# One of two halves gets its own buffers, the gates become plain fp32 and come last: the mixing stage of a two-block network

## The chip, the cores and the metric

One Trainium2 chip, one core. The time is device microseconds of one execution; the median of several runs is compared. The profile is one execution taken by the hardware profiler.

## The reference

A sequence of 256 tokens, width 1024, goes through a first block of two layers (feed-forward, a hybrid attention mixer, feed-forward) and then through a second block, whose mixing sublayer the change is about. It projects the modulated input `u` with one weight matrix `w_in` (1024 x 6032) into columns for three things:

```python
a_lat, b_lat, gates_lat = split(u_lat @ w_in, ...)
oa, _ = gdn_branch(a_lat, state_a)               # gated DeltaNet, 4 heads of 128
ob, _ = rwkv_branch(to_col_major(b_lat), state_b) # RWKV-7, 8 heads of 64
y = (sigmoid(g_a) * (oa @ w_o_a) + sigmoid(g_b) * (ob @ w_o_b)) @ w_out
```

Both branches run over the tokens in two directions and start from states that the same branches computed on a context of 256 tokens. RWKV first mixes each column with its neighbours, `cols + (0.5*(left + right) - cols) * mu`, then builds per token a decay, a key, a removal vector and a value, and runs a linear recurrence. A hierarchical mixture of experts (32 experts, the most of the weights) follows, and a last norm.

## The kernel before

The program is written as Python that emits instructions; a planner orders them. Every instruction has a priority (the order in which the program emits it; `high_priority(n)` puts a stretch ahead by n), and the planner, with its own model of durations, lets each engine take the first ready one. Each engine then runs its list in that fixed order. On-chip memory comes from pools on two stacks ("left", "right"); a tile in a place that was used before waits until the old tile's last reader is done. A tag with `bufs=n` is a ring of n buffers.

Matrix products with weights are done in three matmuls of reduced fp32: `split_w` (L90) makes a high part on ScalarE (L132) and a low part on VectorE (L133), and `mm3` (L99) multiplies low by high, high by low, high by high (L102 to L104). `norm_pair` (L175) gives `u` as such a pair, `hh` and `hl`.

`mix` (L2182) runs the stage. `begin` computes `u` and stores both parts to DRAM as `u_lat`. `rwkv_proj` projects v, k, w, r in this order (15 column blocks of 128; `shifted`, L1399, does the neighbour mix in `evict`). Then `rwkv` (L1434) works on four pairs of heads, in two halves of two pairs. In `rwkv_half` (L1491), `first` (L1506) builds for a pair and a direction the decays (tanh, a scan, two exponentials) and the factors AR and BK; `second` (L1556) multiplies them on TensorE, masks the products on VectorE (L1569 Mak, L1571 Ur, L1574 Mr) and transposes; there are four such stages in a half. Then the 64x64 triangular matrices are inverted (`inverse`, L951: transposes on VectorE, 15 steps of substitution L975 and L977, then products of blocks on TensorE), and a chain of four chunks (L1625 on) carries the state and accumulates the outputs `yr`. `rwkv_out` normalizes a half into `ob`.

All of this has high priority. The buffers AR, BKT, U, R1, Mr and SV exist once, so half 1's writes wait for half 0's readers. Below that priority come, in the order of the program, `gdn_z` and `gdn_proj` (17 blocks; the convolution's taps are L1093), `gates_ahead` (L2217) and `gdn` (L1157). `gates_ahead` computes the 2048 gate columns ahead of their use: 8 groups, each over 8 blocks of `u` reloaded from `u_lat` (L2226), with weights split by ScalarE (L2229) and GpSimd (L2230), the tanh stored to DRAM. `gdn` prepares factors for four heads (L1246), inverts 128x128 matrices by the same `inverse`, and runs two chunks; `gdn_out` gives `oa` (L1760). PSUM has 8 banks: two each for tags "g" and "s" (RWKV), three for "a" (GDN), one for "w" (gates). `merge` (L2251) then multiplies `oa`, `ob` with their output weights (branch a first), scales with the gates, and projects.

The context's RWKV (`ctx_second`) uses the same functions without outputs, beside a feed-forward of the first block.

Of the kernel before, what the change touches and what calls it, by code (L numbers as in the profile page):

```python
# [31 lines left out]
class Core:  # L32
# [142 lines left out]
    def norm_pair(self, pool, x, rs, A, B=None, keep=None, save=None):  # L175
# [7 lines left out]
        for t in range(2):  # L183
# [17 lines left out]
            if save is not None:  # L201
                for i, v in enumerate((hh, hl)):
                    nc.sync.dma_start(out=save[:, i, :, ts], in_=v[:, :, ts].bitcast(F32))
# [719 lines left out]
class Block2:  # L923
    def __init__(self, k, a, rows, pool):
        self.k, self.a, self.R, self.cst = k, a, rows, pool
        tc, nc, ctx = k.tc, k.nc, k.ctx
# [22 lines left out]


    def inverse(self, U, nb, size):  # L951
# [6 lines left out]
        assert nb == B  # L958

        t = pool.tile([P, B, 32], F32, tag="t2", name="Ut", bufs=self.t2)  # L960
        for q in range(4):
            bs, cb = slice(32 * q, 32 * q + 32), 32 * q % size
            nc.vector.transpose(t[bs].rearrange("p a b -> p (a b)"),
                                U[bs, :, cb:cb + 32].rearrange("p n (h c) -> p c h n", h=2))
        W = pool.tile([P, B, B], F32, tag="inv", name="Ub", bufs=3)
        nc.vector.tensor_scalar(W, t[:, :, 0:B], self.halves[:, 0:1], None, op0=OP.mult)
# [35 lines left out]
        pq = bmm("g", B, [(b, U[st[b], :, diag[b]], DD[st[b], :, 0:B]) for b in range(4)])  # L1002
# [8 lines left out]
        pq = bmm("g", 32, [(b + 1, U[st[b], :, off[b]], DD[st[b]]) for b in (0, 2)])  # L1011
        nc.vector.tensor_copy(Q[st[1]], pq[st[1]])
        nc.scalar.activation(Q[st[3]], pq[st[3]], AF.Copy)
        for b in range(4):
            if b % 2:
                nc.gpsimd.tensor_copy(U[st[b], :, diag[b]], DT[st[b]])
            else:
                nc.scalar.activation(U[st[b], :, diag[b]], DT[st[b]], AF.Copy)
# [3 lines left out]
        nc.vector.tensor_copy(U[st[0], :, off[0]], px[st[0]])  # L1022
        nc.scalar.activation(U[st[2], :, off[2]], px[st[2]], AF.Copy)
# [35 lines left out]
    def proj(self, u, w, start, n, evict):  # L1059
# [5 lines left out]
        for f0 in range(0, n, 256):  # L1065
            pg = k.ps("g", [P, 2, T], "pg")
            for g0 in range(f0, min(f0 + 256, n), wide):
                m = min(wide, n - g0)
                wr = k.raw(w[:, start + g0: start + g0 + m].rearrange("(c p) f -> p c f", p=P), [P, KC, m])
                for h0 in range(0, m, P):  # L1070
                    mm = min(P, m - h0)
                    fi = (g0 + h0 - f0) // P
                    for c0 in range(0, KC, cs):
# [83 lines left out]
    def gdn(self, cols, s0, with_out, name, Sout=None):  # L1157
# [88 lines left out]
        def factors(h):  # L1246
# [8 lines left out]
            for dn in range(4):  # L1255
                nc.vector.tensor_scalar(E[:, dn], gb[:, dn], col[:, dn, h:h + 1], 0.0, op0=OP.subtract, op1=OP.min)
            nc.scalar.activation(E, E, AF.Exp)
# [102 lines left out]
class Rwkv(Block2):  # L1360
# [3 lines left out]
    def rwkv_setup(self):  # L1364
# [11 lines left out]
        self.mstr = c.tile([P, 64], F32, name="mstr")  # L1376
        self.minc = c.tile([P, 2, 64], F32, name="minc")
        for h in range(2):
            b = slice(64 * h, 64 * h + 64)
            one = k.ones[b, 0:64]  # L1380
            nc.gpsimd.affine_select(self.mstr[b], one, pattern=[[1, 64]], base=0, channel_multiplier=-1,
                                    compare_op=OP.is_gt, fill=0.0)
            nc.gpsimd.affine_select(self.minc[b, 0], one, pattern=[[1, 64]], base=0, channel_multiplier=-1,
                                    compare_op=OP.is_ge, fill=0.0)
            nc.gpsimd.affine_select(self.minc[b, 1], one, pattern=[[-1, 64]], base=63, channel_multiplier=-1,
                                    compare_op=OP.is_ge, fill=0.0)
        nv = c.tile([P, 12 + 15 + 16], F32, name="rwc")
        self.mu = R["rwkv_mu_2"]
# [10 lines left out]
    def shifted(self, u, w, start, nch, mu0, colmajor, out):  # L1399
# [3 lines left out]
        def evict(i, m, pg):  # L1403
            pad = pool.tile([P, 2, T + 2], F32, tag="t2", name="pad2", bufs=self.t2)
            nc.gpsimd.memset(pad[:, :, 0:T + 2:T + 1], 0.0)
            for j in range(m):
                src, dst = pg[:, j], pad[:, j, 1:T + 1]
                if colmajor:
                    src = src.rearrange("p (r c) -> p c r", r=4)
                    dst = dst.rearrange("p (c r) -> p c r", r=4)  # L1410
                nc.scalar.activation(dst, src, AF.Copy)
            x = pad[:, :m, 1:T + 1]
            s = pool.tile([P, 2, T], F32, tag="t2", name="shs", bufs=self.t2)
            nc.gpsimd.tensor_tensor(s[:, :m], pad[:, :m, 0:T], pad[:, :m, 2:T + 2], op=OP.add)
            nc.vector.scalar_tensor_tensor(s[:, :m], s[:, :m], 0.5, x, op0=OP.mult, op1=OP.subtract)
            for j in range(m):
                nc.vector.scalar_tensor_tensor(out[:, i + j], s[:, j], self.mu[:, mu0 + i + j:mu0 + i + j + 1],
                                               pad[:, j, 1:T + 1], op0=OP.mult, op1=OP.add)
        self.proj(u, w, start, nch * P, evict)

    def rwkv_part(self, name, u, w, colmajor, lows=3):

        start, n, tag = dict(v=(1024, 4, "vT"), k=(512, 4, "kTr"), w=(1536, lows, "lo"), r=(0, 4, "rT"))[name]
        t = self.keep.tile([P, n, T], F32, name=tag)
        self.shifted(u, w, 2064 + start, n, self.MU[name], colmajor, t)
# [4 lines left out]
    def rwkv_proj(self, u, w, colmajor):  # L1430

        return tuple(self.rwkv_part(name, u, w, colmajor) for name in "vkwr")

    def rwkv(self, cols, S0, with_out, name, Sout=None, ob=None):  # L1434


# [8 lines left out]
        kk = pool.tile([P, 4, T], F32, tag="kk", name="kk")  # L1445
# [12 lines left out]
        rkT = pool.tile([72, T], F32, tag="rkT", name="rkT")[64:72]  # L1458
# [5 lines left out]
        out = None  # L1464
        for hf in range(2):

            SV = pool.tile([P, 2, 4, 4, 64], F32, tag="SV", name="SV")
            for d in range(2):
                vh = vT[:, 2 * hf:2 * hf + 2]
                if d == 1:  # L1470
                    vr = pool.tile([P, 2, T], F32, tag="t2", name="vTb", bufs=self.t2)
                    nc.vector.tensor_copy(vr, rev(vh))
                    vh = vr
                for t in range(2):
                    pt = k.ps("s", [P, 2, P], "ptv")
                    for p in range(2):
                        nc.tensor.transpose(pt[:, p], vh[:, p, t * P:(t + 1) * P], k.ident)
                    for q in range(2):
                        for h in range(2):
                            i = pt[64 * q:64 * q + 64, :, 64 * h:64 * h + 64]  # L1480
                            o = SV[64:128, h, 2 * t + q, 2 * d:2 * d + 2]
                            if h == 0:
                                nc.scalar.activation(o, i, AF.Copy)
                            else:
                                nc.vector.tensor_copy(o, i)
            out = self.rwkv_half(hf, kT, rT, lo, kk, SV, None if S0 is None else S0[:, hf],
                           with_out, name + str(hf), None if Sout is None else Sout[:, hf], vT, ob, out)
        if with_out:
            out()

    def rwkv_half(self, hf, kT, rT, lo, kk, SV, S0, with_out, name, Sout, vT, ob, before):  # L1491
# [3 lines left out]
        AR = pool.tile([P, 4, 4, na, 64], F32, tag="AR", name="AR")  # L1495
        BKT = pool.tile([P, 4, nb, P], F32, tag="BKT", name="BKT")
        U = pool.tile([P, 16, 64], F32, tag="U", name="Ur")
        R1 = pool.tile([P, 4, 4, 64], F32, tag="R1", name="R1")
        gam = pool.tile([P, 4, 4], F32, tag="gam", name="gam")
        Mr = None  # L1500
        if with_out:
            Mr = pool.tile([P, 4, 2, 4, 64], F32, tag="Mr", name="Mr")
            bon = pool.tile([P, 2, 4], F32, tag="bon", name="bon")
        kds = {}

        def first(pl, d):  # L1506
# [12 lines left out]
            kd = pool.tile([P, T], F32, tag="kd%d" % d, name="kdr", bufs=2)  # L1519
            nc.vector.tensor_scalar(kd, th[:, 1], self.kah[:, p:p + 1], self.kac[:, p:p + 1],  # L1520
                                    op0=OP.mult, op1=OP.add)
            nc.gpsimd.tensor_tensor(kd, kd, kT[:, p], op=OP.mult)
            kds[pl, d] = kd
            nc.vector.tensor_scalar(th, th, 0.5, 0.5, op0=OP.mult, op1=OP.add)
            nc.gpsimd.tensor_tensor(th[:, 1], th[:, 1], kk[:, p], op=OP.mult)
# [4 lines left out]
            ee = pool.tile([P, 2, 4, 64], F32, tag="t2", name="ee", bufs=self.t2)  # L1530
            ep, em = ee[:, 0], ee[:, 1]
            cum4 = cum.rearrange("p (c t) -> p c t", t=64)
            nc.scalar.activation(ep, cum4, AF.Exp, scale=-EMH)
            nc.scalar.activation(em, cum4, AF.Exp, scale=EMH)
            nc.vector.tensor_copy(gam[:, :, pd], ep[:, :, 63])
# [4 lines left out]
            kkd = nat(kk[:, p])  # L1540
            aa = AR[:, pd, :, 0]
            nc.vector.scalar_tensor_tensor(aa[:, :, 1:], kkd[:, :, 1:], -1.0, ep[:, :, :63],
                                           op0=OP.mult, op1=OP.mult)
            nc.vector.tensor_scalar(aa[:, :, 0:1], kkd[:, :, 0:1], -1.0, None, op0=OP.mult)
            if with_out:
                rv = rT[:, p].rearrange("p (c t) -> p c t", t=64)
                if d == 0:
                    nc.gpsimd.tensor_tensor(AR[:, pd, :, 1], rv, ep, op=OP.mult)
                else:
                    nc.gpsimd.tensor_tensor(AR[:, pd, :, 1], revd(rv, (1,)), revd(ep, (2,)), op=OP.mult)  # L1550
            BK = pool.tile([P, 4, 2, 64], F32, tag="t2", name="BK", bufs=self.t2)
            nc.vector.tensor_tensor(BK[:, :, 0], nat(th[:, 1]), em, op=OP.mult)
            nc.vector.tensor_tensor(BK[:, :, 1], nat(kd), em, op=OP.mult)
            return BK

        def second(pl, d, BK):  # L1556

            pd = 2 * d + pl
            bs = [slice(0, 64), slice(64, P)]
# [871 lines left out]
```

## Time and profile before

| | |
|---|---|
| median of 3 runs | 2396.19 us (2391.33 to 2402.87) |
| profiled execution | 2390.7 us, its span 2389.0 us |
| TensorE (matmul) busy | 2249.9 us (94%), 19065 instructions |
| VectorE | 1689.7 us (71%) |
| ScalarE | 1199.8 us (50%) |
| GpSimd | 344.1 us (14%) |
| mean granted TensorE clock | 0.953 |

The clock is a share of full speed (1.00 is 2.4 GHz, 0.50 is 1.2 GHz). PE is TensorE, PEld its weight load, DVE VectorE, ACT ScalarE, POOL GpSimd, SP the engine that issues most DMAs. A matmul's recorded duration holds its way through the array, so durations overlap, and spacing tells the rate. A matmul of plain fp32 operands leaves two records, one of the reduced kind one. The mixing stage runs from 1616 us, when the first block ends, to about 2053 us; the experts follow to the end.

### The profile page before, as it was taken

How to read it: one execution, taken by the hardware profiler on the slowest of the kernel's cores; microseconds unless marked ns; L12 is line 12 of the kernel's file. 1: busy time of each engine (PE TensorE's matmuls, PEld its weight loads, DVE VectorE, ACT ScalarE, POOL GpSimd, SP SyncE). 2: the span in 40 equal slices, each digit the busy share in tenths (PEclk: the TensorE clock that was granted, in tenths of full speed). 3: DMA queues.
4: the chain of work that ended last, by engine and by line, in shares of the span. 5: the costliest groups of instructions: out<-in, count | busy, mean ns of one | idle time of the engine just before them, and what ended most of it. 6: DMA issues, size and time to landing. Idle time of an engine off the chain costs nothing. (4 is left out here: it accounts for less than half of the span.)

```text
span 2389.0 us, 46279 instructions
## 1 busy us (share of the span) xinstructions
PE 2249.9 (94%) x19065; PEld 2041.7 (85%) x19065; DVE 1689.7 (71%) x2796; ACT 1199.8 (50%) x1919; POOL 344.1 (14%) x465
## 2 busy tenths in 40 slices
PE   7999999999999999999999999998989887899997
PEld 6999988897889888888888979998877777799996
DVE  6775575766665674675856668886885866789997
ACT  5554455555443543544554554443553313477775
POOL 2000112121200100100122210002245511000000
PEclk9999999999999989999999999998988668899999
DMA  9676344455434334342545468986445415699992
GB/s 327 223 248 202 111 150 143 140 166 188 142 125 163 132 112 152 128 142 68 173 130 166 143 211 299 331 285 185 125 133 161 146 40 193 239 374 351 353 352 98
DMA packets 325166, 450.91 MB, mean 189 GB/s; under 512 B 16122, under 2 KB 253236, under 8 KB 324564
## 3 DMA queue, kind: packets, MB, share of 16 engines
q1 hardware_dynamic: 324276, 447.06, 55.9%
q8 instruction: 152, 2.49, 0.4%
q0 software_dynamic: 672, 0.82, 0.3%
q14 instruction: 66, 0.54, 0.1%
HBM read 438.09 MB, written 9.76 MB: 187 GB/s over the span
## 5 line engine op out<-in xcount | busy, mean ns | idle before, releaser
L133 DVE TENSOR_TENSOR wl<-raw,wh 128x1024 fp32r<-128x1024 f32 (+1 forms) x703 | 860.0, 1230 | 364.4 <-ACT wh L132 355.2
L132 ACT ACTIVATE wh<-raw 128x1024 fp32r<-128x1024 f32 (+1 forms) x703 | 730.5, 1043 | 465.8 <-PE pg L104 189.5
L102 PE MATMUL pg<-hh,wl 128*128 128x256 f32 x2176 | 627.9, 289 | 4.9 <-DVE wl L133 4.4
L103 PE MATMUL pg<-hl,wh 128*128 128x256 f32 x2176 | 625.9, 288 | 0.4 <-DVE hl L133 0.4
L104 PE MATMUL pg<-hh,wh 128*128 128x256 f32 x2176 | 625.8, 288 | 0.0
L102 PEld LDWEIGHTS pg<-hh,wl 128*128 128x128 f32 x2176 | 420.1, 193 | 17.2 <-issue 6.0
L103 PEld LDWEIGHTS pg<-hl,wh 128*128 128x128 f32 x2176 | 420.0, 193 | 11.1 <-issue 6.6
L104 PEld LDWEIGHTS pg<-hh,wh 128*128 128x128 f32 x2176 | 420.1, 193 | 7.8 <-issue 6.4
L102 PE MATMUL ph<-wh,m0t 128*128 128x256 f32 x512 | 146.4, 286 | 0.0
L102 PE MATMUL acc<-wh,ul 128*128 128x512 f32 x352 | 137.9, 401 | 8.7 <-DVE ul L133 7.0
L103 PE MATMUL ph<-wl,m0t 128*128 128x256 f32 x512 | 144.2, 282 | 0.1
L104 PE MATMUL ph<-wh,m0t 128*128 128x256 f32 x512 | 143.7, 281 | 0.0
L104 PE MATMUL acc<-wh,uh 128*128 128x512 f32 x352 | 140.7, 400 | 0.0
L103 PE MATMUL acc<-wl,uh 128*128 128x512 f32 x352 | 140.4, 399 | 0.0
L103 PE MATMUL acc<-wl,hh 128*128 128x512 f32 (+2 forms) x320 | 120.5, 377 | 0.0
L104 PE MATMUL acc<-wh,hh 128*128 128x512 f32 (+2 forms) x320 | 120.4, 378 | 0.0
L102 PE MATMUL acc<-wh,hl 128*128 128x512 f32 (+2 forms) x320 | 116.9, 381 | 0.5 <-DVE hl L133 0.5
L103 PEld LDWEIGHTS ph<-wl,m0t 128*128 128x128 f32 x512 | 96.5, 189 | 1.2 <-DVE wl L133 0.4
L104 PEld LDWEIGHTS ph<-wh,m0t 128*128 128x128 f32 x512 | 96.5, 188 | 0.5
L102 PEld LDWEIGHTS ph<-wh,m0t 128*128 128x128 f32 x512 | 96.7, 189 | 0.1
L454 ACT ACTIVATE sg<-pg 128x256 f32<-128x256 f32 x80 | 30.8, 385 | 127.4 <-PE pg L104 123.8
L1705 DVE SCALAR_TENSOR_TENSOR adacc<-raw,silu_c,adacc 128x512 f32<-128x512 f32 x112 | 83.4, 747 | 15.3 <-DMA raw<-in_ada_w_dram 14.7
(712 smaller groups left out, 4214.5 us busy)
## 6 DMA issues: line engine op xcount, KB each, us to landing
raw<-in_ffn_w_gu_dram SPq DMA_DIRECT2D x88, 1024.0 KB
raw<-in_w_in_dram SPq DMA_DIRECT2D x56, 1024.0 KB
raw<-in_ffn_w_down_dram SPq DMA_DIRECT2D x44, 1024.0 KB
raw<-in_w_gate_dram SPq DMA_DIRECT2D x32, 1024.0 KB
raw<-in_moe_w_gate_dram SPq DMA_DIRECT2D x32, 1024.0 KB
raw<-in_moe_w_up_dram SPq DMA_DIRECT2D x32, 1024.0 KB
raw<-in_moe_w_down_dram SPq DMA_DIRECT2D x32, 1024.0 KB
raw<-in_ada_w_dram SPq DMA_DIRECT2D x48, 512.0 KB
```

The lines of the kernel that those rows point to most:

```text
L102: t.matmul(out, lhs[1], rhs[0], start=start, stop=False)
L103: t.matmul(out, lhs[0], rhs[1], start=False, stop=False)
L104: return t.matmul(out, lhs[0], rhs[0], start=False, stop=stop)
L132: return (nc.scalar.activation(h, src, AF.Copy), nc.vector.tensor_tensor(l, src, h.bitcast(F32), op=OP.subtract))
L133: nc.vector.tensor_tensor(l, src, h.bitcast(F32), op=OP.subtract))
L454: nc.scalar.activation(sg, pg[:, 0], AF.Silu)
L1705: nc.vector.scalar_tensor_tensor(acc, wv, sc, acc, op0=OP.mult, op1=OP.add)
```

## The change

Six things, all in the second block. (1) RWKV's halves: `rwkv_half` takes its buffers from a pool given to it, builds factors and products at once and returns a function `solve` for the rest; the two halves' pools are separate, the second laid where the projections' memory was. Solves have priorities of their own. (2) Gates: `norm_pair` also adds the two parts of `u` to a full fp32 tile `uf` on GpSimd, the gates use plain fp32 matmuls on unsplit weights, `u_lat` goes, and they are emitted after GDN. (3) Masked products: the two halves of heads are laid so that one operation masks all (`UM`, `mask2`). (4) Factors: key and removal factor as one tile `X`, the first column of AR without an operation of its own; the shift as `out*(1-mu) + 0.5*mu*(left+right)`. (5) In the mixing stage (`lean`) several scalings and GDN's subtraction move from VectorE to ScalarE. (6) Order and rings: w, k, r, v; `gdn_proj` before `gdn_z`; the projections' split weights have 2 buffers, not 3.

```diff
 norm_pair:
+            if full is not None:
+                nc.gpsimd.tensor_tensor(full[:, js, ts], hh[:, js, ts].bitcast(F32), hl[:, js, ts].bitcast(F32), op=OP.add)
 inverse (U becomes at(b), one tile for each half of partitions):
-        nc.vector.tensor_scalar(W, t[:, :, 0:B], self.halves[:, 0:1], None, op0=OP.mult)
+        self.scaled(W, t[:, :, 0:B], self.halves[:, 0:1])      # ScalarE if lean, else VectorE
-            for h in range(2):
-                nc.vector.tensor_scalar(t[:, :, B * h:B * h + B], yv, self.halves[:, h:h + 1], None, op0=OP.mult)
+            nc.vector.tensor_scalar(t[:, :, 0:B], yv, self.halves[:, 0:1], None, op0=OP.mult)
+            self.scaled(t[:, :, B:], yv, self.halves[:, 1:2])
 gdn factors, if lean:
-                nc.vector.tensor_scalar(E[:, dn], gb[:, dn], col[:, dn, h:h + 1], 0.0, op0=OP.subtract, op1=OP.min)
+                    nc.scalar.activation(E[:, dn], gb[:, dn], AF.Relu, scale=-1.0, bias=col[:, dn, h:h + 1])
 shifted:
                 nc.scalar.activation(dst, src, AF.Copy)
+                nc.scalar.activation(o, src, AF.Copy, scale=self.mu1[:, mu0 + i + j:mu0 + i + j + 1])
-            nc.vector.scalar_tensor_tensor(s[:, :m], s[:, :m], 0.5, x, op0=OP.mult, op1=OP.subtract)
 rwkv_half, first:
-            nc.gpsimd.tensor_tensor(kd, kd, kT[:, p], op=OP.mult)
-            nc.vector.tensor_scalar(th, th, 0.5, 0.5, op0=OP.mult, op1=OP.add)
-            nc.gpsimd.tensor_tensor(th[:, 1], th[:, 1], kk[:, p], op=OP.mult)
+            for o, i in ((f[:, 0], th[:, 1]), (th[:, 0], th[:, 0])):
+                if self.lean:
+                    nc.scalar.activation(o, i, AF.Copy, scale=0.5, bias=0.5)
...
+            for h in range(2):
+                o = X[hb[h]]
+                nc.gpsimd.tensor_tensor(o if h == 0 else revd(o, (1,)), f[hb[h]], kkT[hb[h], p], op=OP.mult)
-            nc.vector.tensor_copy(gam[:, :, pd], ep[:, :, 63])
+            nc.scalar.activation(gam[:, :, pd], cum4[:, :, 63], AF.Exp, scale=-EMH)
-            nc.vector.tensor_tensor(BK[:, :, 0], nat(th[:, 1]), em, op=OP.mult)
-            nc.vector.tensor_tensor(BK[:, :, 1], nat(kd), em, op=OP.mult)
+            nc.vector.tensor_tensor(BK.rearrange("p c j t -> p j c t"), Xn if d == 0 else revd(Xn, (2, 3)),
+                                    em.unsqueeze(1).to_broadcast([P, 2, 4, 64]), op=OP.mult)
 rwkv_half, second:
-                nc.vector.tensor_tensor(Mak[64:128], pm[64:128, :, 0], ..., op=OP.mult)
-                nc.vector.tensor_tensor(U[b, 4 * pd:4 * pd + 4], pm[0:64, :, 0], ..., op=OP.mult)
-                    nc.vector.tensor_tensor(Mr[:, pd, h], pm[:, :, 1], ..., op=OP.mult)
+                nc.vector.tensor_tensor(UM[h][:, 4 * pd:4 * pd + 4], pm,
+                                        self.mask2[:, d, 0:na].unsqueeze(1).to_broadcast([P, 4, na, 64]), op=OP.mult)
 mix:
-            wp = Weights(proj.enter_context(k.pool("uw", "right")), 2048, 2, 1024, 3)
+            wp = Weights(proj.enter_context(k.pool("uw", "right")), 2048, 2, 1024, 2)
                 with k.tc.high_priority(100000):
-                    self.rwkv(cols, self.Sb, True, "rl", None, ob)
+                    kk = self.rwkv_keys(cols, True)
+                    solve = [half(0, seta)]
                 with k.use(**G), k.pool("gp", "right") as self.pool:
-                    self.gdn_z(u, w, oa)
                     gcols = self.gdn_proj(u, w, True)
+                    self.gdn_z(u, w, oa)
             proj.close()
+            setb = right.enter_context(k.pool("rb", "right"))
+            with k.tc.high_priority(100000), k.use(**G):
+                solve.append(half(1, setb))
+            with k.tc.high_priority(200000):
+                solve[0]()
+            with k.tc.high_priority(100000):
+                solve[1]()
-            with k.pool("gm", "right") as self.pool, k.use(W=Weights(gf, 256, 4, 256, 2), **G):
-                self.gates_ahead(gf, a["w_in_2"][0][:, 3984:6032])
+            with k.pool("gm", "right") as self.pool, k.use(W=Weights(gf, 512, 4, 0, 0), **G):
                 self.gdn_out(self.gdn(gcols, self.Sa, True, "gl"), oa)
+                self.gates_ahead(a["w_in_2"][0][:, 3984:6032])
 gates_ahead:
-                    u = pool.tile([P, 2, 2, T], F32, tag="u", name="u", bufs=2)
-                    nc.sync.dma_start(out=u, in_=self.u_lat[:, :, c:c + 2])
-                nc.scalar.activation(ws[0], wr, AF.Copy)
-                nc.gpsimd.tensor_tensor(ws[1], wr, ws[0].bitcast(F32), op=OP.subtract)
-                    k.mm3(pg[:, j], ...)
+                    nc.tensor.matmul(pg[:, j], wr[:, c % 2, j * P:j * P + P], self.uf[:, c],
+                                     start=c == 0 and j == 0, stop=c == KC - 1 and j == 1)
```

The context's RWKV takes (3) and (4) too, with the scalings left on VectorE.

## Rows read from the trace of the kernel before

**Rows 1.** Windows: us, then busy us (instructions) of PE, PEld, DVE, ACT, POOL; clock, DMA
```profile
1635.00:1755.00 120.00, 116.96 (x953) 109.94 (x951) 91.90 (x164) 60.46 (x104) 34.22 (x39) 0.99 0.44 133
1755.00:1858.00 103.00, 86.44 (x1274) 74.96 (x1273) 65.67 (x158) 42.96 (x125) 53.51 (x65) 0.87 0.59 176
1858.00:1922.00 64.00, 52.13 (x424) 44.76 (x423) 54.05 (x113) 20.92 (x51) 30.46 (x41) 0.70 0.42 123
1922.00:1995.00 73.00, 62.71 (x1460) 56.58 (x1459) 43.37 (x110) 13.99 (x39) 6.11 (x10) 0.71 0.23 74
1995.00:2053.00 58.00, 47.84 (x281) 42.55 (x282) 39.80 (x42) 22.78 (x29) 9.34 (x9) 0.87 0.71 248
```

**Rows 2.** Windows of 10 us, where two inverses' small matmuls run alone
```profile
1940.00:1950.00 10.00, 8.63 (x418) 8.37 (x411) 3.14 (x8) 0.00 (x0) 0.00 (x0) 0.50 0.28 104
```

**Rows 3.** Timeline of VectorE (start us, us, ...): first and last of each half's preparation
```profile
1702.96 0.41 DVE L1520 TENSOR_SCALAR kdr<-th,rwc 128x256 f32<-128x256 f32 x1
...
1757.09 0.43 DVE L1574 TENSOR_TENSOR Mr<-pm,minc 128x256 f32<-128x256 f32 x1
...
1863.49 0.41 DVE L1520 TENSOR_SCALAR kdr<-th,rwc 128x256 f32<-128x256 f32 x1
...
1914.53 0.42 DVE L1574 TENSOR_TENSOR Mr<-pm,minc 128x256 f32<-128x256 f32 x1
```

**Rows 4.** Timeline of TensorE: half 0's last outputs, which read SV and Mr
```profile
1847.40 0.97 PE L1619 MATMUL yr<-SV,Mr 128*64 128x64 f32 x16
```

**Rows 5.** Timeline of VectorE: GDN's inverse and output; from 1922.35 half 1's inverse
```profile
1857.67 0.69 DVE L1268 TENSOR_TENSOR U<-Eb,pk 128x512 f32<-128x512 f32 x1
...
1868.49 0.14 DVE L975 TENSOR_TENSOR Pb<-Ub,Yb 128x1 f32<-128x1 f32 x1
...
1900.47 0.38 DVE L977 TENSOR_REDUCE Yb<-Pb 128x15 f32<-128x225 f32 x1
...
1921.95 0.47 DVE L1003 TENSOR_SCALAR Q<-ps_inv,halves 128x256 f32<-128x256 f32 x1
1922.35 0.15 DVE L975 TENSOR_TENSOR Pb<-Ub,Yb 128x1 f32<-128x1 f32 x1
...
1935.19 0.39 DVE L977 TENSOR_REDUCE Yb<-Pb 128x15 f32<-128x225 f32 x1
...
1941.58 0.48 DVE L1003 TENSOR_SCALAR Q<-ps_inv,halves 128x256 f32<-128x256 f32 x1 [0.74 <-PE ps_inv L996]
...
1953.83 0.68 DVE L1045 COPY U<-ps_inv 64x512 f32<-64x512 f32 x1 [1.64 <-PE ps_inv L1044]
...
1994.34 0.75 DVE L1760 SCALAR_TENSOR_TENSOR oa<-pt,rowcols,oa 128x512 f32<-128x512 f32 x1 [0.72 <-PE pt L1758]
```

**Rows 6.** Timelines of TensorE and ScalarE: the end of half 1's output, then branch b
```profile
2009.18 0.66 PE L1807 MATMUL pt<-ident,yrw 128*128 128x128 f32 x4 [3.06 <-DVE yrw L1803]
...
2009.65 0.66 ACT L1809 ACTIVATE ob<-pt 128x256 f32<-128x256 f32 x2 [2.39 <-PE pt L1807]
...
2013.65 0.55 PE L102 MATMUL pb<-o,wl 128*128 128x256 f32 x1 [3.82 <-DVE merged L251]
```

**Rows 7.** The projections' matmuls by tile: ns min/median/max, first and last start
```profile
L104 PE MATMUL pg<-hh,wh x256: 277/283/420, 1634.4 to 1755.0; 128*128 128x256 f32 x124, 128*16 128x256 f32 x4
```

**Rows 8.** Window with the gates' matmuls alone (those that read tile u)
```profile
1755.00:1922.00 167.00, 69.83 (x376) 0.80 0.52 156
```

**Rows 9.** Plain fp32 matmuls of 128x128 by 256: by line, then two in sequence
```profile
L804 PE MATMUL sbs<-sbw,m_lt x16: 377/379/382, 376.8 to 1228.0; 128*128 128x256 f32 x16
...
376.78 0.60 PE L804 MATMUL sbs<-sbw,m_lt 128*128 128x256 f32 x2
```

**Rows 10.** Groups by form, 1615 to 2000 us: xcount | busy us, mean ns | idle before
```profile
L2230 POOL TENSOR_TENSOR wl<-raw,wh 128x256 fp32r<-128x256 f32 x64 | 50.0, 785 | 61.6 <-ACT wh L2229 59.3 <-issue 2.1
L133 DVE TENSOR_TENSOR wl<-raw,wh 128x1024 fp32r<-128x1024 f32 x34 | 42.7, 1261 | 22.5 <-ACT wh L132 22.4
L132 ACT ACTIVATE wh<-raw 128x1024 fp32r<-128x1024 f32 x34 | 35.7, 1055 | 19.4 <-PE pg L104 13.9 <-DVE kk L1449 3.6 <-DMA raw<-in_w_in_dram 1.8
L1569 DVE TENSOR_TENSOR Mak<-pm,mstr 64x256 f32<-64x256 f32 x16 | 6.8, 428 | 3.7 <-PE pm L1563 3.3
L1574 DVE TENSOR_TENSOR Mr<-pm,minc 128x256 f32<-128x256 f32 x16 | 6.6, 415 | 0.1
```

More of the change, by code (lines that the diff above doesn't have):

```diff
@@ L173, in rms, with norm_pair @@
         return self.pow(pool, v, "%sr%d" % (name, t))
-    def norm_pair(self, pool, x, rs, A, B=None, keep=None, save=None):
+    def norm_pair(self, pool, x, rs, A, B=None, keep=None, full=None):
         nc = self.nc
@@ L1072, in proj @@
                     fi = (g0 + h0 - f0) // P
+                    if not isinstance(u, (tuple, list)):
+                        for c in range(KC):
+                            k.nc.tensor.matmul(pg[:mm, fi], wr[:, c, h0:h0 + mm], u[:, c], start=c == 0, stop=c == KC - 1)
+                        continue
                     for c0 in range(0, KC, cs):
@@ L1463, in rwkv @@
             nc.vector.tensor_tensor(kk[:, p], kk[:, p], pb, op=OP.mult)
-        out = None
+        return kk
+    def rwkv(self, cols, S0, name, Sout):
+        kk = self.rwkv_keys(cols, False)
         for hf in range(2):
[L1467 to L1487, printed above, removed]
@@ L1488, in rwkv, with rwkv_half @@
-        if with_out:
-            out()
-    def rwkv_half(self, hf, kT, rT, lo, kk, SV, S0, with_out, name, Sout, vT, ob, before):
-        k, nc, pool, R = self.k, self.k.nc, self.pool, self.R
+            self.rwkv_half(hf, cols, kk, S0, False, name + str(hf), Sout[:, hf], None, self.pool)()
+    def rwkv_half(self, hf, cols, kk, S0, with_out, name, Sout, ob, sets):
+        k, nc, pool, R = self.k, self.k.nc, self.pool, self.R
+        vT, kT, lo, rT = cols
+        S0 = None if S0 is None else S0[:, hf]
+        kkT = kT
+        SV = sets.tile([P, 2, 4, 4, 64], F32, tag="SV", name="SV")
+        for d in range(2):
+            vh = vT[:, 2 * hf:2 * hf + 2]
+            if d == 1:
+                vr = pool.tile([P, 2, T], F32, tag="t2", name="vTb", bufs=self.t2)
+                nc.vector.tensor_copy(vr, rev(vh))
+                vh = vr
+            for t in range(2):
+                pt = k.ps("s", [P, 2, P], "ptv")
+                for p in range(2):
+                    nc.tensor.transpose(pt[:, p], vh[:, p, t * P:(t + 1) * P], k.ident)
+                for q in range(2):
+                    for h in range(2):
+                        i = pt[64 * q:64 * q + 64, :, 64 * h:64 * h + 64]
+                        o = SV[64 - 64 * h:128 - 64 * h, h, 2 * t + q, 2 * d:2 * d + 2]
+                        if h == 0:
+                            nc.scalar.activation(o, i, AF.Copy)
+                        else:
+                            nc.vector.tensor_copy(o, i)
@@ L1604, in rwkv_half @@
         second(*last)
-        if before is not None:
-            before()
-        XT = self.inverse(U, 16, 64)
-        if with_out:
-            gate = self.rwkv_gate(hf, bon, vT, lo[:, 2])
-        if with_out:
-            yp = [k.ps("g", [P, 2, 2, 64], "yr") for _ in range(2)]
-        def outputs(c, lhs, rhs, first, last):
-            for d in range(2):
-                cn = 3 - c if d else c
-                for pl in range(2):
-                    for h in range(2):
-                        nc.tensor.matmul(yp[h][64 * (cn % 2):64 * (cn % 2) + 64, cn // 2, pl], lhs(h, 2 * d + pl),
-                                         rhs(h, 2 * d + pl), start=first and pl == 0, stop=last and pl == 1)
@@ L1670 @@
+        return solve
 class Tail(Rwkv):
@@ L2089, in ctx_store @@
         if c is not None:
-            self.ctx[name] = self.dram.tile(list(c.shape), F32, name="c" + c.name)
+            c = c[:, :, 1] if name == "k" else c
+            self.ctx[name] = self.dram.tile(list(c.shape), F32, name="c%s" % name)
             self.k.nc.sync.dma_start(out=self.ctx[name], in_=c)
@@ L2104, in ctx_load @@
             if d is not None:
-                t = self.keep.tile(list(d.shape), F32, name="cl%s" % i)
-                self.k.nc.sync.dma_start(out=t, in_=d)
+                n = list(d.shape)
+                t = self.keep.tile(n[:2] + [2] + n[2:] if i == "k" else n, F32, name="cl%s" % i)
+                self.k.nc.sync.dma_start(out=t[:, :, 1] if i == "k" else t, in_=d)
             out.append(t)
```

272 lines of the change are left out of this document (146 added, 126 removed).

## The prediction

> **What bounds the kernel now.** I read the page's busy shares and its 40 slices first: TensorE is busy nearly everywhere, and the slices where it and its clock fall lie between two thirds and nine tenths of the span. That is the mixing stage of the second block, the only place where the change alters the order of work. Then I read this stage by parts [rows 1]. From 1635 to 1755 us the projections run: TensorE is busy 117.0 of 120 us at clock 0.99, VectorE 91.9. From 1755 to 1995 us it is another regime: TensorE 201.3 of 240 us (86.4 + 52.1 + 62.7), VectorE 163.1, ScalarE 77.9, the clock only 0.70 to 0.87, and at 0.50 where chains of small matmuls run alone [rows 2]. No engine is full there. What ends this part is two chains: the second RWKV half, and gated DeltaNet (GDN) with its triangular inverse.
>
> The VectorE timeline shows why they are late. Half 0's factors and products run from 1703 to 1757, half 1's only from 1863 to 1915 [rows 3]. They are the same work, but half 1 writes the buffers that half 0 reads until 1848.4 [rows 4]. It so falls on top of GDN's inverse. GDN's last product is written at 1857.7; the 15 steps of its substitution take from 1868.5 to 1900.9, because half 1's instructions stand between them; the next result is used at 1922.0. Half 1's own inverse, with nothing between, needs 1922.4 to 1935.6 for the steps, and is at that same point at 1941.6. GDN's last correction is written at 1954.5, its output ends at 1995.1 [rows 5], and half 1's output ends later still, at 2010.3 [rows 6].
>
> **The change part by part.** The profiled execution took 2390.7 us (its span 2389.0 and 1.7 around it); the sum is made against it. The median of the runs is 2396.19, 0.2% more.
>
> *Separate buffers.* Half 1 gets its own set, laid where the projections' input and weights were, so it can start when their last matmul ends, at 1755.0 [rows 7], not 1863: some 105 us earlier. What is late next is GDN, so only its part of the collision counts. The steps shrink from 32.4 us (1868.5 to 1900.9) to the 13.2 us of half 1's own: 19.2. The stretch from there to the next use shrinks from 21.1 to 6.0: 15.1. Together **-34**.
>
> The following block products (1922.0 to 1954.5, 32.5 us) ran at clock 0.5 beside half 1's inverse. At the higher of the two clock levels (2.4 against 1.2 GHz) they could take half, without any change they take the same: 0 to -16. I take **-8**: the gates, which now come last, will lie between them and keep TensorE at work, but half 1's solve may still be near.
>
> *GDN's preparation (1768 to 1858)* loses the gates' matmuls and gets half 1's preparation beside it instead, with three PSUM banks for both and RWKV first. The gates hold TensorE for 69.8 us between 1755 and 1922 [rows 8]; half 1's preparation is 53 us long now. VectorE has room: 65.7 of 103 us busy [rows 1]. I take 0, bounds -20 and +53 (all of half 1's preparation put in front).
>
> *Half 1's output.* The merge waits for it now: TensorE stands idle 3.1 and 3.8 us for its last steps [rows 6]. With half 1 done first this goes: **-7**.
>
> *Gates in plain fp32.* They were 128 products of three matmuls; a 128x256 one takes 0.12 us at full clock (953 in 117.0 us [rows 1]), so 46 us. A plain fp32 product of this shape is recorded as two matmuls: one lasts 0.38 us, two together 0.60, so each adds 0.22 [rows 9]. 128 x 2 x 0.22 = 56 us. TensorE gets 10 us more, and since it must now fit into a shorter stretch I count all of it: **+10** (bounds 0, hidden, and +56, all at the end). The loss of 64 splits, 50.0 us on GpSimd [rows 10], and of the reloads of the input counts nothing: neither engine nor queue ends this stage. On SP the gates now issue 32 loads of weights and 8 stores, emitted after GDN; the merge's first weights stand behind them in that queue, which costs nothing while the gates are done before GDN, and belongs to the first rival if not.
>
> The Trainium skill, page "Perfetto Trace Analysis", section "Engine Utilization", puts the output rate of an fp32 matmul at half the usual one. Taken per product that would make the gates cheaper, an estimated 28 us, and the sum 28 us lower. The trace agrees per matmul (0.22 against 0.12) but shows two per product, so I stay with the row.
>
> *Projections.* Three buffers for split weights become two. Each part is split by ScalarE in 1.06 us and then VectorE in 1.26 [rows 10], 2.3 in sequence, while TensorE needs 24 x 0.12 = 2.9 for a part. The slack is 0.6 us, and VectorE is 77% busy [rows 1]: a part that meets a group of RWKV's operations waits. If each of GDN's 17 parts lost 2 us it is +34; if the planner fills the holes with gates, nothing. I take 0: the gates are plain matmuls that need no split and can fill them, and the projections then hand work forward.
>
> *VectorE's smaller work.* The shift loses one of its operations (7), each of the 8 stages loses 8 of 14 (the masked products go from six to two), 9 scalings and 16 subtractions move to ScalarE (busy 60.5 of 120 and 43.0 of 103 us [rows 1]). That is 96 operations less, 40 us at the 0.42 us of a 128x256 one [rows 10]; 24 that remain double in length, at 0.69 for 128x512 [rows 5] 6 us back: 34 us less. In the projections TensorE's 117 of 120 us hides it; later it is in the terms above. Bounds 0 and -15. GpSimd's new products work on half the partitions: between once and twice the 0.8 us that it takes for as many elements [rows 10], at most 6 us in half 1, which is no longer the last chain.
>
> The Trainium skill, page "SBUF — State Buffer", section "Who interferes with whom", says that a VectorE operation with two SBUF inputs waits for a GpSimd operation that reads SBUF. By it the 50.0 us of removed splits would give VectorE something back beyond this list; no row here separates it, and the sum leaves it out.
>
> The context's RWKV, beside the first block's feed-forward, gets the same edits; TensorE bounds it: -5 to +5, taken as 0. The four full-precision adds in the norm are 0, at most +3: GpSimd is idle there.
>
> Sum: -34 - 8 - 7 + 10 = -39, so 2390.7 - 39 = **2352 us**.
>
> **The rivals.**
>
> *TensorE becomes the bound.* Without the gates it has 201.3 - 69.8 = 131.5 us after 1755; with the new ones at full clock 187. If its idle time stays (240 - 201.3 = 38.7) and the clock too, the part ends at 1755 + 226 = 1981: -14, and -7 for the merge, 2370. If a third of the gates is left over after GDN (19 us), 2389. For it: busy already 84%. Against: denser work had the higher clock in this trace (0.99 against 0.70). 2370 to 2390.
>
> *Full overlap.* At full clock the 131.5 us become about 101, with the gates 157; with 10 us idle the part ends at 1922: -73 - 7, 2311. For it: VectorE needs only some 130 us. Against: GDN's chain alone, 1768 to 1858 as now, then inverse and output without company, does not end so soon.
>
> *GDN comes last (slower).* Half 1's preparation, first by priority, takes the three shared banks, and GDN's preparation waits its whole 53 us. It decides from about 40 us on. 53 - 34 - 8 - 7 + 10 = +14: 2405, and up to 2439 if the two split buffers cost their 34 too. For it: the banks, and priorities that put GDN behind all RWKV work. Against: VectorE and TensorE both have room from 1768 to 1858.
>
> *The change does less than it says:* the planner leaves half 1 where it was, since the memory it takes is given free late. Then only +10 remains: 2401.
>
> **How the numbers follow.** Forecast 0.46 (its own range 2330 to 2370); TensorE the bound 0.2; full overlap 0.12; GDN last 0.15; half 1 not earlier 0.07. Within 0.5% (2384 to 2408, about what a measurement of this kernel can tell from no change): a third of the TensorE case, all of the last, and a fifth of GDN last: 0.17. Slower: the rest of GDN last, with the two buffers' cost, 0.12. Faster: 0.71. For 8 in 10 the range is cut inside the full overlap and inside GDN last: 2312 to 2406.
>
> **What would show it.** Right: half 1's masked products before 1820, its output before GDN's, GDN's substitution in under 18 us, gates still on TensorE after GDN's inverse, merge starting near 1955, clock above 0.8 there. Wrong: gates after GDN's output (TensorE bound); GDN's product later than 1890 (GDN last); TensorE idle for the weights' split in the projections (two buffers too few); half 1 starting after 1850.

## The result, and the profile after

The changed kernel takes 2410.9 us (median of 8 runs, 2407.1 to 2416.5) against 2397.7 (2391.3 to 2402.9): 1.0059 times the time before, interval 1.0046 to 1.0072. It is slower by 13 us; 2352 was forecast. The profiled executions lie further apart, 2416.5 and 2390.7 us, at opposite ends of their runs, so of the 26 us between the traces about half is difference between executions.

Landmarks of the two timelines (start, us) split these 26 us:

| landmark | before | after | stretch to it, after minus before |
|---|---|---|---|
| normed input is split (first `hl`) | 1632.1 | 1644.8 | +12.7 |
| GDN's first operation (`G`) | 1768.3 | 1849.8 | +68.8 |
| GDN's first product with its state (`pks`) | 1953.7 | 1990.4 | -44.8 |
| merge's first product (`pb`) | 1996.5 | 2027.3 | -5.9 |
| router's first product (`prt`) | 2062.3 | 2084.3 | -8.8 |
| end of the span | 2389.0 | 2414.8 | +3.8 |

The windows of the mixing stage after the change, cut at its own events (columns as in [rows 1]): projections; half 0's solve with half 1's preparation; GDN's preparation; its inverse; its output; merge.

```profile
1645.00:1790.00 145.00, 131.80 (x1005) 122.86 (x1005) 98.26 (x174) 72.68 (x140) 43.22 (x50) 0.93 0.34 103
1790.00:1850.00 60.00, 45.78 (x991) 38.69 (x993) 37.16 (x75) 19.87 (x52) 21.41 (x26) 0.72 0.04 9
1850.00:1945.00 95.00, 87.98 (x1157) 70.89 (x1156) 49.33 (x112) 28.39 (x89) 24.32 (x24) 0.95 0.31 86
1945.00:1990.00 45.00, 30.94 (x682) 27.20 (x682) 24.90 (x62) 8.11 (x17) 3.72 (x6) 0.66 0.13 43
1990.00:2027.00 37.00, 26.57 (x157) 24.17 (x155) 17.59 (x40) 8.02 (x25) 3.03 (x5) 0.68 0.21 68
2027.00:2084.00 57.00, 50.78 (x295) 45.19 (x296) 42.53 (x47) 24.18 (x32) 9.50 (x6) 0.92 0.95 336
```

No engine is full; TensorE comes nearest in the third window (88.0 of 95 us). The second is new: 60 us in which TensorE is busy three quarters at clock 0.72, hardly a DMA runs (share 0.04), and GDN has not begun. VectorE's timeline of GDN, to set against [rows 5]:

```profile
1849.80 0.17 DVE L1182 TENSOR_TENSOR G<-pab,dtb 128x8 f32<-128x8 f32 x1
...
1943.11 0.69 DVE L1283 TENSOR_TENSOR U<-Eb,pk 128x512 f32<-128x512 f32 x1
...
1949.52 0.16 DVE L983 TENSOR_TENSOR Pb<-Ub,Yb 128x1 f32<-128x1 f32 x1
...
1962.05 0.39 DVE L985 TENSOR_REDUCE Yb<-Pb 128x15 f32<-128x225 f32 x1
...
1969.26 0.48 DVE L1011 TENSOR_SCALAR Q<-ps_inv,halves 128x256 f32<-128x256 f32 x1 [2.28 <-PE ps_inv L1004]
...
1990.50 0.68 DVE L1053 COPY U<-ps_inv 64x512 f32<-64x512 f32 x1 [1.02 <-PE ps_inv L1052]
...
2024.77 1.41 DVE L1783 SCALAR_TENSOR_TENSOR oa<-pt,rowcols,oa 128x512 f32<-128x512 f32 x2 [1.00 <-PE pt L1781]
```

The substitution takes 12.9 us (1949.5 to 1962.4), the stretch to the next use 6.9: the collision is gone, as forecast. But the first row stands at 1849.8. What happens just before it on TensorE:

```profile
1842.08 0.42 PE L1177 MATMUL pab<-ident,ab 16*128 16x16 f32 x4
...
1847.52 0.46 PE L1642 MATMUL yr<-Sr,AR 64*64 64x64 f32 x13
...
1849.36 0.92 PE L1642 MATMUL yr<-SV,UM 128*64 128x64 f32 x16 [0.48 <-ACT SV L1659]
```

GDN's first product (`pab`) is there at 1842.1, in PSUM; its first write to SBUF, `G`, follows half 0's last read of `AR` (1847.5 to 1848.0). In the built program `G` lies at bytes 94,400 to 94,464 of each partition and half 0's `AR` at 93,920 to 102,112. GDN's pool now takes 94,400 to 155,520, over half 0's set (85,728 to 128,832); before, it took 137,504 to 198,624, the room that the projections leave. Half 1's new set (155,520 to 198,624) has pushed it out.

### The profile page after: what moved, and what is told of

Same layout as the page of the kernel before. It is cut to its first block, busy times and chain, and to the rows that moved or that the text cites. A ratio compares the mean times of both kernels' runs of the same rounds, so it can differ in the third digit from the quotient of the medians.

```text
span 2414.8 us, 45622 instructions
## 1 busy us (share of the span) xinstructions
PE 2268.7 (94%) x18937; PEld 2049.2 (85%) x18937; DVE 1644.4 (68%) x2664; ACT 1192.7 (49%) x1921; POOL 326.2 (14%) x427
```

## The experiments

The times of before are 2395 to 2398 in each group of runs; ratios are to it.

**Whose wait it is.** *One set*, with GDN's buffers back in the projections' room (and one scratch pool for both halves and a weight buffer of the gates less, which makes them fit):

```
-            setb = right.enter_context(k.pool("rb", "right"))
...
-                solve.append(half(1, setb))
+                solve.append(half(1, seta))
```

> Theory (the wait only changed hands): in the changed kernel GDN's buffers lie over half 0's, so GDN's preparation starts at 1849.8 instead of 1768.3, after half 0's last use, and that 69 us (counted from the stage's start) eats the 45 us by which GDN's chain got shorter. With one RWKV set again, and GDN's buffers back in the room of the projections, GDN's first operation comes some 60 us earlier, its substitution is again mixed with half 1's preparation, and the time is 2390 to 2405, 5 to 20 us below the changed kernel. Rival (the separate sets are worth the predicted 34 to 49 us, and something else, gates or two split buffers, costs 50): the time rises to 2435 to 2460.

Measured: 2455.3 us, 1.025 (1.022 to 1.028). The time is the rival's, but not its reason: GDN began later still, at 1905.8. This kernel leaves half 1's preparation on GDN's three PSUM banks and emits it first; TensorE's timeline has GDN's first product right behind half 1's last:

```profile
1903.04 1.11 PE L1599 MATMUL p<-SV,UM 64*64 64x64 f32 x8
1904.08 0.61 PE L1177 MATMUL pab<-ident,ab 16*128 16x16 f32 x4
```

*One set on its own banks* takes only that away:

```
-            with k.tc.high_priority(100000), k.use(**G):
+            with k.tc.high_priority(100000):
                 solve.append(half(1, seta))
```

> The one-set kernel, which took 2455 us, with half 1's preparation on RWKV's own PSUM banks, as in the kernel before, instead of GDN's three. Theory (banks go round in the order in which the code asks for them, so GDN's first tile waited there for half 1's last one and GDN began at 1905.8): GDN begins at 1780 to 1790 and the time falls by 40 to 60 us, to 2395 to 2415. The separate sets as written are then worth no more than 10 us. Rival (GDN's late start came from half 1's priority, not from its banks): it still begins after 1880 and the time stays above 2435.

Measured: 2403.0, 1.0025 (1.0011 to 1.0040), 52 us less, and GDN begins with the projections' end (below). The theory holds: banks asked for earlier in the code held GDN. This kernel is 8 us faster than the changed one (1.0059), from which it differs in half 1's set, scratch and banks and in one weight buffer of the gates: the separate sets, as written, cost time.

*Without half 1*, in two kernels of the same work; in the first an unused buffer of half 1's size keeps GDN over half 0's set, in the second GDN has the free room:

```
-                solve.append(half(1, setb))
+            k.nc.gpsimd.memset(ob[:, 2:4], 0.0)
...
+            hole = setb.tile([P, 10776], F32, name="hole")    # first kernel only
```

> The changed kernel without RWKV's half 1 (its output set to zero), with an unused buffer of the same size in its place, so that GDN's buffers lie over half 0's as they do in the changed kernel. It is the partner of the next run. Theory: GDN's first operation stays behind half 0's last use, at about 1830 to 1845. Rival (GDN is late because RWKV's work has priority and shares three PSUM banks with it): without half 1 GDN starts within a few us of the projections' end, 1790 to 1800.

> The same work as the run before it, instruction for instruction; only the addresses of GDN's buffers differ: they lie in the room that the projections leave. Theory: GDN's first operation comes at 1785 to 1795, 40 to 55 us sooner than in the run before, and the time falls by 30 to 50 us. Rival (priority and banks): GDN's start and the time stay within 5 us of the run before.

Measured: 2372.7 (0.989, 0.986 to 0.993) and 2339.1 (0.975, 0.972 to 0.978): 34 us for addresses alone, of GDN's buffers and of the gates' result buffer among them (first gate eviction at 1835.0 and 1789.9). GDN's last `G` (last start in each row: kernel before, changed, without half 1 over half 0's set, the same in free room, one set, one set on its own banks), each from the view by tile of its own kernel:

```profile
L1170 DVE TENSOR_TENSOR G<-pab,dtb x4: 155/164/167, 582.6 to 1770.1; 128x8 f32<-128x8 f32 x4
```
```profile
L1182 DVE TENSOR_TENSOR G<-pab,dtb x4: 155/161/166, 577.5 to 1851.4; 128x8 f32<-128x8 f32 x4
```
```profile
L1182 DVE TENSOR_TENSOR G<-pab,dtb x4: 155/160/167, 582.6 to 1835.7; 128x8 f32<-128x8 f32 x4
```
```profile
L1182 DVE TENSOR_TENSOR G<-pab,dtb x4: 155/160/166, 581.6 to 1790.6; 128x8 f32<-128x8 f32 x4
```
```profile
L1182 DVE TENSOR_TENSOR G<-pab,dtb x4: 156/162/167, 576.9 to 1906.8; 128x8 f32<-128x8 f32 x4
```
```profile
L1182 DVE TENSOR_TENSOR G<-pab,dtb x4: 156/162/167, 579.5 to 1786.5; 128x8 f32<-128x8 f32 x4
```

The third and fourth rows are 45 us apart with no half 1 in either: half 0's memory is enough to hold GDN. The kernel without half 1 over half 0's set shows it by itself: GDN's first product (`pab`) stands in PSUM from 1785, and `G` follows only at 1834.2, behind half 0's last reads of `AR`:

```profile
L1177 PE MATMUL pab<-ident,ab x4: 208/208/229, 1785.3 to 1785.5; 16*128 16x16 f32 x4
L1642 PE MATMUL yr<-Sr,AR x48: 218/219/365, 1822.3 to 1832.1; 64*64 64x64 f32 x48
L1182 DVE TENSOR_TENSOR G<-pab,dtb x2: 155/161/167, 1834.2 to 1835.7; 128x8 f32<-128x8 f32 x2
```

In the changed kernel the banks were free at 1842 and the memory at 1848; the memory came last, by 6 us.

**Who slows GDN once it runs.** *GDN ahead of half 1*: `with k.tc.high_priority(150000):` around its call.

> The changed kernel with GDN's preparation, inverse and output ahead of half 1 in priority. Half 1's output is done at 1967 in the changed kernel and GDN's at 2026. Theory (GDN is now the only late chain and is held up by half 1's solve): its last correction, 1990 now, comes 10 to 25 us sooner, 2386 to 2401. Rival (GDN's own steps and the gates on TensorE set its pace): within 4 us of the changed kernel.

Measured: 2396.9, 0.9999 (0.9982 to 1.0015): 14 us less than the changed kernel, a time in the theory's range. Its mechanism shows in part: counted from the stage's start (the first `hl`), `pks` comes 6.4 us sooner and not 10 to 25. From `G` to the merge's first product it took 170.7 us instead of 177.5; half 1's output ended at 346 instead of 324 us of the stage, still ahead of the merge (373). Where the rest of the 14 us comes from was not found.

*No gates*: the loop of products replaced by a copy of other numbers into their buffer.

> The changed kernel without the gates' products (their buffer is filled with other numbers). Theory (the gates lie in TensorE's idle time and GDN's chain waits for small steps): 2396 to 2408, under 15 us gained of the 56 us of matmuls. Rival (TensorE, busy all of the time from 1890 to 1950, is the bound of GDN's preparation there): 2360 to 2382.

Measured: 2387.2, 0.9967 (0.9951 to 0.9983): 22 us less, between the two; neither holds as put. From `G` to `pks` GDN takes 115.0 us instead of 140.6. So the gates hold GDN up for 26 us. Yet none of them runs from 1668 to 1850: their 2 KB result buffer `gth` lies in GDN's pool. Two kernels move it: *beside their weights* (then they may run from the start of the stage), and *in a pool of its own* at the same address, opened earlier (then from the projections' end); two more add the other edits.

```
-            th = self.pool.tile([P, 2, T], F32, tag="gth", name="gth")
+            th = k.W.pool.tile([P, 2, T], F32, tag="gth", name="gth")   # beside the weights
+            th = self.gt.tile([P, 2, T], F32, tag="gth", name="gth")    # own pool
```

> The changed kernel with the gates' result buffer beside their weights (three raw buffers instead of four), so that no gate waits for GDN's pool. The planner then orders 106 of the 128 products ahead of the projections' last matmul. Theory A (the gates fit into TensorE's waits in the projections): GDN's first operation stays within 5 us of 205 from the stage's start, its chain falls from 141 to about 115, 2384 to 2394. Theory B (they displace projections: 106 products of 0.4 us are 42 us, TensorE's waits there some 20): GDN begins 15 to 25 us later and the time is 2398 to 2412.

> The changed kernel with the gates' result buffer at its old address but in a pool of its own, opened before half 0's set is given up. Theory (the pool held the gates for 182 us): some 60 of the products run between the projections' end and GDN's start, on a TensorE that idles 24 of 60 us there, GDN's chain falls by 8 to 15 us and the time to 2396 to 2403. Rival (a product beside half 0's solve costs that solve as much as it saves GDN): 2408 to 2414.

Measured: 2409.6, 1.0058 (1.0041 to 1.0076), and 2417.4, 1.0093 (1.0066 to 1.0121). Theory B holds for the first; the second is as slow as its rival said and 3 us slower still. The evictions of the gates (changed kernel, beside the weights, own pool) moved as meant, the second column of times the first and last start:

```profile
L2272 ACT ACTIVATE gth<-pg x8: 578/590/598, 1850.6 to 1959.6; 128x512 f32<-128x512 f32 x8
```
```profile
L2272 ACT ACTIVATE gth<-pg x8: 583/597/601, 1670.0 to 1853.7; 128x512 f32<-128x512 f32 x8
```
```profile
L2273 ACT ACTIVATE gth<-pg x8: 591/598/598, 1785.5 to 1888.3; 128x512 f32<-128x512 f32 x8
```

GDN's stretch from `G` to `pks` fell from 140.6 to 113.6 and 125.0, and its start moved from 205.0 to 228.9 and 223.2 us of the stage. Against the kernel without gates they cost 22 to 30 us in each of these three places. A reading that fits: half 0 and GDN now stand in one row, so what the gates no longer take from GDN they take from the work before it.

**The other parts.** *Two buffers of split weights in the kernel before*: its `Weights(..., 2048, 2, 1024, 3)` with 2 at the end.

> The kernel before with two buffers of split weights in the second block's projections instead of three, nothing else. Theory: the projections lose the 9 us that the changed kernel's TensorE idles more for the weights' split (13.3 against 4.4 us for the whole kernel, on L102), so 2400 to 2410. Rival (the slack of 0.6 us a part suffices and the longer projections come from gates drawn into them): 2395 to 2400.

Measured: 2406.6, 1.0047 (1.0032 to 1.0063): 11 us. The idle time that the weights' split ended in the projections (1640 to 1790) is 13.6 us here, 19.9 in the changed kernel, 23.1 in the one-set kernel on its own banks, and not in the list of the kernel before. These lists add up the waits of the weight loads and of the matmuls, which can be the same stretch; the matmuls alone wait 6.5, 9.0 and 10.4 us:

```profile
  DVE wl L133: 13.6, 10
```
```profile
  DVE wl L133: 19.9, 15
```
```profile
  DVE wl L133: 23.1, 19
```

*Half-size parts*: `Weights(..., 2048, 2, 512, 4)` in the changed kernel.

> The changed kernel with the projections' weights split in parts of 512 columns in four buffers, the same bytes as two of 1024. Theory (two buffers leave one part of head start, which a group of VectorE work uses up): three parts of head start instead of one bring back 7 to 11 of the 11 us that two buffers cost the kernel before, so 2400 to 2404. Rival (the serial split by ScalarE and VectorE is itself too slow beside the convolutions): 2408 to 2414.

Measured: 2415.6, 1.0067 (1.0041 to 1.0094), 2 us above the rival's range. More, smaller parts bring nothing back; the rival's reason was not tested.

*The context's RWKV as before*, in the changed kernel:

> The changed kernel with the context's RWKV of the kernel before (its operations and its six scratch buffers). Theory (the context's new RWKV is slower and runs 5 to 10 us into the first block's work): 2400 to 2405. Rival (the first block's 10 to 16 us in the profiles are differences from execution to execution): 2408 to 2413.

Measured: 2401.5, 1.0012 (0.9995 to 1.0030): 9 us less than the changed kernel. The profiles of the first block agree. The second block's norm begins at 1611.3 to 1626.6 us in the eight profiles with the old context (mean 1619.5) and at 1623.3 to 1636.8 in the ten with the new one (mean 1631.6). (The mixing stage gives a part back in this run's profile: from the first `hl` to the router's first product it takes 446.6 us, 439.5 in the changed kernel.) Four of them, changed kernel, without gates, context as before, plain gates in the kernel before:

```profile
L189 DVE TENSOR_TENSOR xn<-x,am x4: 681/682/683, 1632.5 to 1635.6; 128x512 f32<-128x512 f32 x4
```
```profile
L189 DVE TENSOR_TENSOR xn<-x,am x4: 680/682/683, 1628.2 to 1631.2; 128x512 f32<-128x512 f32 x4
```
```profile
L189 DVE TENSOR_TENSOR xn<-x,am x4: 680/684/685, 1620.3 to 1623.3; 128x512 f32<-128x512 f32 x4
```
```profile
L189 DVE TENSOR_TENSOR xn<-x,am x4: 679/682/683, 1620.7 to 1623.7; 128x512 f32<-128x512 f32 x4
```

*Plain gates in the kernel before*, in their old place:

```
-                    k.mm3(pg[:, j], (ws[0][:, js], ws[1][:, js]), ...
+                    nc.tensor.matmul(pg[:, j], wr[:, c % 2, j * P:j * P + P], self.uf[:, c], ...
```

> The kernel before with its gates as plain fp32 products, emitted where they were, and nothing else. Theory of the prediction (two records of 0.22 us a product instead of three of 0.12: 10 us more TensorE, of which beside GDN's preparation a part is hidden): 2397 to 2407. Rival (the splits on ScalarE and GpSimd and the reloads were themselves a wait for GDN's steps): 2385 to 2394.

Measured: 2393.2, 0.9980 (0.9967 to 0.9992): 5 us faster, in the rival's range. Its reason is not borne out: from `G` to `pks` GDN takes 201.4 us here and 185.5 in the kernel before, and the stage up to the router's first product takes 429.5 and 430.2, so the profiles don't show where the 5 us lie. The gates' matmuls keep TensorE busy 63.3 us there, 69.8 before [rows 8], same window:

```profile
1755.00:1922.00 167.00, 63.34 (x252) 50.47 (x252) 0.00 (x0) 0.82 0.21 60
```

It is the only version with all of the work whose interval lies wholly below the kernel before.

**Do the parts add up?** *GDN ahead and the context as before*; the same two on the gates beside their weights, and on their own pool; and *one set with three buffers* and the context as before.

> The changed kernel with both edits that gave something back: GDN ahead of half 1 in priority (14 us) and the context's RWKV of the kernel before (9 us). Theory (the two lie in different stages and add up): 2384 to 2392, below the kernel before. Rival (a part of one is differences between executions, or the planner gives it back): 2394 to 2402.

> The run before with GDN ahead of half 1 and the context's RWKV of the kernel before. If the parts add up, 23 us less than the run before: 2361 to 2371 by theory A, 2375 to 2389 by theory B. If only the larger of the two counts, as in the earlier run with both, 14 less: 2370 to 2380 or 2384 to 2398.

> The run before with GDN ahead of half 1 and the context's RWKV of the kernel before. If the edits add up (12 + 14 + 9): 2373 to 2382. If GDN's priority and the gates' hold are the same gain counted twice: 2386 to 2392.

> One RWKV set on its own banks (2403 us), with the context's RWKV of the kernel before (9 us) and three buffers of split weights again (11 us in the kernel before). What is left of the change is its fewer VectorE operations and the plain gates after GDN. Theory (the three add up): 2379 to 2388. Rival (the plain gates, which need no split, fill the projections' holes, so the third buffer gives nothing here): 2391 to 2396.

Measured: 2397.2 (0.9996, 0.9981 to 1.0011), 2395.6 (0.9999, 0.9984 to 1.0013), 2396.3 (1.0002, 0.9986 to 1.0018) and 2393.5 (0.9985, 0.9971 to 1.0000). The first is the rival's, though its first block is shorter; the second and third give 14 and 21 of the 23 us, the third from 2417, so that it ends above both its ranges; the last is in its rival's range. Every change makes the planner order the mixing stage anew, and with intervals of 3 to 4 us on each side it stays open whether the effects overlap or the orders differ by luck.

## Why the prediction was wrong

The step that failed is *separate buffers*, in its sentence "Half 1 gets its own set, laid where the projections' input and weights were, so it can start when their last matmul ends". It asked what half 1 gains from that room and not who had used it. GDN had. With *GDN's preparation* at 0 the sum left its start where it was, at 1768; it starts 69 us later in the stage. By the landmarks 5 us of this are longer projections (the last operation on GDN's columns starts 141.1 instead of 136.1 us into it) and 64 the wait. The bound of +53 was drawn from PSUM banks; the wait was longer and came from memory. The diff shows it without a trace: GDN's pool is opened after half 0's set is closed, on the side where half 1's set has just been put. What the step would bring if GDN kept its room is not shown: no run has two sets and GDN clear of both.

The rival *GDN comes last*, at 0.15, has the right outcome (2405 to 2439; it is 2411) and half of the reason: the banks it named do hold GDN, until 1842, 6 us less than the memory, and alone they cost 52 us in the one-set kernel. In the changed kernel they were not tried by themselves. That its 2405 comes so near is luck in part: the wait was longer than its 53 us and had another cause.

The other steps, in order:
- *Substitution and the stretch behind it*, -34: right. 32.4 became 12.9 us and 21.1 became 6.9, together -33.7.
- *Block products*, -8: 32.5 became 21.9 us (1969.3 to 1991.2), -10.6, but not by a higher clock: it is 0.50 there, as in [rows 2]. What went is half 1's work between them.
- *GDN's preparation*, 0: as a length right. 1849.8 to 1949.5 is 99.7 us; 1768.3 to 1868.5 was 100.2.
- *Half 1's output*, -7: right, the merge is 8.8 us shorter.
- *Gates*, +10: wrong in both ways. Their form costs nothing and, in their old place, the kernel with it is 5 us faster (plain gates in the kernel before); TensorE is busy 6 us less with them, since the old ones took 0.19 us a matmul in that window (69.8 for 376 [rows 8]) and not 0.12. Without them the changed kernel is 22 us faster; what they cost altogether in their old place was not measured, so the price of the new place stays open. The Trainium skill (page "Perfetto Trace Analysis", section "Engine Utilization") halves the output rate for FP32_LOW_HIGH, which the prediction took for fp32; taken per product that gives an estimated 28 us, and the trace has 63.3.
- *Projections*, 0 (+34 at most): 11 us, from two buffers in the kernel before. In the changed kernel their last matmul starts 143.7 us into the stage instead of 122.9; GDN's columns, now projected before `gdn_z`, come only 5 us later, but half 1 can't start at the 1755 of the prediction.
- *VectorE's smaller work*, hidden: it fits. From the first `hl` to the router's first product VectorE has 96 operations less, as counted (505 instead of 601), and is busy 270.0 us instead of 305.9. The one-set kernel with three buffers has it and gains 4 us, no more than plain gates alone; that is a comparison of two kernels that differ in order too.
- *The context*, 0 (-5 to +5): 9 us, outside its bounds; the reason given there, "TensorE bounds it", did not keep it at 0. Which of its edits it is was not tried.

Of the signs, half 1's masked products began before 1820 (1803.9), its output (done at 1969) came before GDN's, and the substitution was short. Wrong were the merge's start at 2027, the clock of 0.66 and 0.68 from 1945 to 2027, and the gates that ended at 1960, ahead of GDN's block products. Two of its signs of being wrong came: GDN's product later than 1890 (1943), and TensorE idle for the weights' split.

In runs: two buffers +11, context +9, separate sets as written +8 (against one set on its own banks), plain gates -5: together 23, and the change measures 13. Gates behind GDN and fewer VectorE operations were not measured alone; whether they give the 10 back or the parts overlap stays open.

## What to carry to other kernels

When a buffer set is doubled, list what lay in the room that it takes, and for each of those where it lies now and whose last read frees it: a wait that vanishes from one chain may stand on the next. Do the same with PSUM banks, which here went round in the order in which the code asks for them, whatever the priorities (GDN began at 1905.8 us behind half 1 on the same banks, at 1784.7 with half 1 on others). And price a stage by its longest row of dependent chains: half 0 and GDN ran side by side before and stand in one row now, and on that row the gates cost 22 us.

## What the runs showed of the hardware

In two stretches of small matmuls of the changed kernel the granted clock was at the lower level (0.50, 1.2 GHz) although TensorE is recorded busy three quarters of the time: half 0's block products and half 1's products (first row), and GDN's block products (second). Before the second, with gates beside GDN's steps, it was 0.95 from 1850 to 1945:

```profile
1800.00:1815.00 15.00, 11.11 (x412) 10.00 (x412) 7.11 (x12) 2.77 (x9) 5.50 (x6) 0.50 0.04 12
1965.00:1990.00 25.00, 18.65 (x610) 17.56 (x611) 7.87 (x15) 3.95 (x8) 1.76 (x4) 0.50 0.02 4
```

With gates between GDN's steps the clock was 0.86 from 1850 to 1990, without them 0.66 from 1848 to 1963, and GDN's chain was still 26 us longer with them: they cost it more than the clock gave back. That small matmuls stand behind gates on TensorE would explain it; it was not measured by itself. And the first block differs between executions: the four profiles with the changed kernel's first block and the old context RWKV reach its end at 1611.3 to 1624.1 us. One profile of each kernel can't tell a change of 10 us there; eight against ten could.
